# Seven-product output projection of a hybrid decoder layer: the order of the second round's products, of VectorE's steps at the change of rounds, and of the last two pairs

## The chip, the cores and the metric

One core of a Trainium2 chip runs one launch of the kernel. The metric is the device time in microseconds; three runs of the kernel before gave 846.16, 846.9 and 846.91, so its median is 846.9 us. A profiled execution is a run of its own, and its time is given beside these.

In the profile PE is TensorE's matrix multiplication, PEld its weight load, DVE is VectorE, ACT is ScalarE, POOL is GpSimd and SP is the engine that issues most loads.

## The reference, cut to what matters

A layer mixes tokens in three branches and then applies a SwiGLU feed-forward block. The change lies in the last line, for 512 tokens, 1024 channels and 2816 hidden units in float32:

```python
hf = rms_norm(x, ffn_norm_g[l]) @ w_ffn_in[l]
gt, up = jnp.split(hf, 2, axis=-1)
x = x + (jax.nn.silu(gt) * up) @ w_ffn_out[l]
```

## The kernel before, in words

A float32 operand is kept as two rounded parts, hi and lo, and a product of two operands as three matrix multiplications: hi by hi, hi by lo, lo by hi (`mm3`, L92). To split a weight block, ACT casts the hi part (L81) and then DVE subtracts it from the block for the lo part (L82). The hi parts lie in buffers `wh` and the lo parts in `wl`, three of each. `raw` (three buffers) holds a block as it was loaded, and `tt` (two buffers) holds sums of blocks.

The hidden units are done in two calls, of 12 and of 10 tiles of 128. In each, `ffn_in` makes the hidden activations and `ffn_out` (L806) multiplies them with the output weights. `ffn_out` takes the hidden tiles in pairs: six pairs in the first call, five in the second, which ends the kernel. A pair times its two rows of weights is a 2 by 2 block product, and it is done with seven products of half size in place of eight (Strassen and Winograd). The halves of the tokens and the halves of the output columns make four quarters of the output; `x(i, c)` is a 128-token tile `i` and a column half `c` of the running output. Each product writes two banks of PSUM with three matmuls each, so it takes six matmuls.

There are two rounds over all pairs of a call, since eight banks do not hold all sums:

- Round one (L827) makes products 1, 6 and 7 of each pair, into the banks p1, p6 and p7.
- Change of rounds (L845 to L856): ACT copies p1 out (L850), DVE adds p6 to it (L851) and gets s2; ACT writes s2 into the banks p5 (L852), as the start of product 5's sum. DVE adds p7 to the output (L854) and overwrites p7 with minus p7 minus s2 (L855), as the start of product 4's sum. The banks of p6 become p3, those of p7 become p4.
- Round two (L857) makes products 2, 3, 5 and 4 of each pair. Products 2 and 3 use the pair's raw second row of weights, split in one piece. I call that block R, with the pair's number behind it: R0, R1 and so on. Products 5 and 4 use sums that DVE forms (L865 to L867) and that are then split in one piece; I call that block S, likewise S0, S1. Of a pair's 24 matmuls twelve use R and twelve use S.
- After round two, `add` (L877) adds the banks to the output. In the last call the result goes into a new buffer `t` (six of them) and from there to memory by a DMA that ACT issues (L881). For two of the eight tiles ACT copies the bank out (L889) and POOL adds.

PE's instructions run in the order in which the program writes them. The others are put in order by a scheduler, engine by engine, by priorities: what stands in a `high_priority` block (the loads, splits and sums of weights) is put as early as the scheduler finds it ready; `issue_after` puts an instruction behind a named one of its engine. Each engine then works strictly through its row and waits at the first instruction that is not ready. A buffer is given out again once all that reads it is done.

## Time and profile before

| What | Value |
|---|---|
| median of 3 runs | 846.9 us (846.16 to 846.91) |
| the profiled execution, its own time | 846.77 us |
| its span, first to last instruction | 845.0 us |
| PE busy | 822.5 us, 97% of the span |
| DVE busy | 603.8 us, 71% |
| ACT busy | 396.3 us, 47% |
| POOL busy | 37.6 us, 4% |
| mean granted TensorE clock | 0.998 |

The profiled execution's own time is 1.77 us above its span, for what lies around the instructions. In a timeline each row gives the start and the duration in microseconds, then engine, line, operation and what it writes from what it reads; a bracket at its end names the idle time ahead of it on that engine and what ended it. A matmul row's duration is modelled and longer than the distance to the next one, since matmuls are pipelined. In a table by windows "x" is the number of instructions, and the DMA share is the mean busy share of the 16 DMA engines.

### The profile page before, as it was taken

The page shows a single profiled execution, that of the slowest core. Times are in us where ns is not written, and L with a number is a line of the kernel's source. Part 1 is how long each engine was busy: PE and PEld are TensorE (multiplying, and loading weights), DVE is VectorE, ACT ScalarE, POOL GpSimd, SP SyncE. Part 2 cuts the span into 40 slices and gives each one's busy share as a digit, 9 for nine tenths or more (in the row PEclk, how much of TensorE's full clock was granted, in tenths as well). Part 3 has the DMA queues.
Part 4 walks back from the last instruction along what each step waited for, and adds up shares of the span by engine and source line. Part 5 has one row for each costly group of instructions (what it writes and reads, how often), then busy time and mean ns, then how long its engine had stood idle before and what let it go on. Part 6 is the DMA issues. An engine that isn't in the chain of part 4 may idle for free. (4 is left out here: it accounts for less than half of the span.)

```text
span 845.0 us, 9697 instructions
## 1 busy us (share of the span) xinstructions
PE 822.5 (97%) x3727; PEld 682.4 (81%) x3727; DVE 603.8 (71%) x880; ACT 396.3 (47%) x583; POOL 37.6 (4%) x62
## 2 busy tenths in 40 slices
PE   6999999999999999999999999999998999999986
PEld 6888887888888888888888888888886888888864
DVE  5598799897899999774443456556698755566984
ACT  5336698886664222663342353333344323333441
POOL 3100010002100000000000120000000000000001
PEclk9999999999999999999999999999999999999999
DMA  7333114112113143142253133322355432323432
GB/s 250 103 100 96 55 50 150 50 56 95 50 50 100 55 145 100 53 148 99 100 184 115 50 100 100 100 100 88 112 173 185 164 99 100 101 88 112 162 125 100
DMA packets 71274, 90.11 MB, mean 107 GB/s; under 512 B 1920, under 2 KB 56380, under 8 KB 71228
## 3 DMA queue, kind: packets, MB, share of 16 engines
q1 hardware_dynamic: 70060, 87.39, 31.2%
q10 hardware_dynamic: 1168, 2.10, 0.6%
q8 instruction: 29, 0.48, 0.2%
q14 instruction: 17, 0.14, 0.1%
HBM read 87.39 MB, written 2.10 MB: 106 GB/s over the span
## 5 line engine op out<-in xcount | busy, mean ns | idle before, releaser
L90 PE MATMUL mm<-u,wh 128*128 128x512 f32 x1536 | 474.8, 390 | 0.0
L90 PEld LDWEIGHTS mm<-u,wh 128*128 128x128 f32 x1536 | 287.4, 188 | 59.4 <-DVE u L710 0.6
L90 PE MATMUL mm<-u,wl 128*128 128x512 f32 x768 | 299.2, 390 | 0.0
L81 ACT CAST wh<-raw 128x1024 fp32r<-128x1024 f32 (+1 forms) x154 | 146.9, 954 | 284.8 <-PE mm L90 219.2
L82 DVE TENSOR_TENSOR wl<-raw,wh 128x1024 fp32r<-128x1024 f32 (+1 forms) x152 | 168.4, 1109 | 61.9 <-ACT wh L81 61.5
L90 PEld LDWEIGHTS mm<-u,wl 128*128 128x128 f32 x768 | 144.2, 188 | 30.0
L502 DVE SCALAR_TENSOR_TENSOR cf<-cf,cols_w,cf 128x512 f32<-128x512 f32 x120 | 89.9, 749 | 3.7 <-ACT cf L500 1.2
L793 DVE TENSOR_TENSOR t<-mm,cf 128x512 f32<-128x512 f32 x22 | 15.2, 691 | 59.7 <-PE mm L90 59.7
L90 PE MATMUL mm<-m,wh 128*128 128x512 f32 x128 | 39.4, 389 | 0.0
L90 PE MATMUL mm<-wh,m 128*128 128x512 f32 x104 | 35.0, 392 | 4.1 <-DVE t L851 2.7
L81 ACT CAST wh<-tt 128x1024 fp32r<-128x1024 f32 x22 | 23.1, 1052 | 24.3 <-PE mm L90 24.3
L82 DVE TENSOR_TENSOR wl<-tt,wh 128x1024 fp32r<-128x1024 f32 x22 | 26.9, 1222 | 10.6 <-ACT wh L81 10.5
L791 DVE TENSOR_TENSOR t<-mm,cf 128x512 f32<-128x512 f32 x22 | 15.1, 688 | 24.8 <-PE mm L90 24.8
L90 PE MATMUL z<-wh,m 128*128 128x512 f32 x84 | 30.4, 396 | 2.0 <-DVE z L855 2.0
L90 PEld LDWEIGHTS mm<-m,wh 128*128 128x128 f32 x128 | 24.0, 188 | 4.9
L78 ACT ACTIVATE s<-s 128x384 f32<-128x384 f32 (+1 forms) x48 | 26.9, 561 | 1.2
L90 PEld LDWEIGHTS mm<-wh,m 128*128 128x128 f32 x104 | 19.5, 188 | 9.4 <-DVE t L851 3.5
L90 PE MATMUL mm<-m,wl 128*128 128x512 f32 x64 | 24.9, 389 | 0.0
L448 DVE SCALAR_TENSOR_TENSOR s<-z,s 128x384 f32<-128x384 f32 (+1 forms) x24 | 14.4, 598 | 11.6 <-ACT s L78 10.4
L78 ACT ACTIVATE t<-t 128x512 f32<-128x512 f32 x31 | 19.6, 631 | 3.7 <-DVE t L791 3.7
L717 POOL TENSOR_TENSOR cf<-cf,t 128x512 f32<-128x512 f32 x7 | 9.9, 1415 | 255.2 <-ACT t L715 255.0
L558 DVE TENSOR_TENSOR t<-mm,t 128x512 f32<-128x512 f32 x16 | 10.9, 689 | 14.0 <-PE mm L90 14.0
(257 smaller groups left out, 1070.3 us busy)
## 6 DMA issues: line engine op xcount, KB each, us to landing
raw<-in_w_in_dram SPq DMA_DIRECT2D x23, 1024.0 KB
raw<-in_w_ffn_in_dram SPq DMA_DIRECT2D x22, 1024.0 KB
raw<-in_w_ffn_out_dram SPq DMA_DIRECT2D x11, 1024.0 KB
raw<-in_w_ffn_out_dram SPq DMA_DIRECT2D x11, 512.0 KB
raw<-in_w_in_dram SPq DMA_DIRECT2D x10, 512.0 KB
raw<-in_w_o_dram SPq DMA_DIRECT2D x4, 1024.0 KB
raw<-in_w_ffn_out_dram SPq DMA_DIRECT2D x11, 256.0 KB
m<-in_x_dram SPq DMA_DIRECT2D x8, 256.0 KB
```

The source lines that it names most:

```text
L78: table(nc.scalar.activation(o, i, f, **kw))
L81: (copy or nc.scalar.copy)(hi, src)
L82: (sub or nc.vector.tensor_sub)(lo, src, hi.bitcast(F32))
L90: nc.tensor.matmul(o, lhsT, rhs, start=start, stop=stop, skip_group_check=True)
L448: marks.append(nc.vector.scalar_tensor_tensor(t, z, 0.0, t, ALU.max, ALU.add))
L502: nc.vector.scalar_tensor_tensor(y, pad[:, n:n + S], w(n), y, ALU.mult, ALU.add)
L558: nc.vector.tensor_mul(s[0], y, s[0])
L717: nc.gpsimd.tensor_add(sumsq, sumsq, s)
L791: nc.vector.tensor_mul(g, pg[0], rstd[0])
L793: nc.vector.tensor_mul(u, pu, rstd[0])
```

## The change

Round two's order on PE: products 2 and 3 of a pair are followed by products 5 and 4 of the pair before it, not of the same pair. In the last call, the last two pairs are done product by product: 5 of both, then 3, 4 and 2 of both. The last pair's R and S are split there into buffers `u`, which held the input of `ffn_in` and are free by then, and not into `wh` and `wl`.

At the change of rounds, ACT copies p7 out first (`s7`), DVE overwrites p7 at once and adds the copy to the output later; all of this but the last addition gets a high priority. From the second pair on, the sums of a pair are put behind a named instruction of DVE: behind the overwriting of the second bank of p7, and then behind the sums of the pair before it.

At the end, all additions are DVE's and stand in place: no buffer `t`, no copy by ACT, no addition by POOL, and the DMAs read the output's own tiles. The additions come in the order 5, 3, 4, 1 in the last call, and 1, 3, 5, 4 in the first.

```diff
--- before.py
+++ after.py
@@ -812,12 +812,17 @@
                 a = [t[:, i * P:(i + 1) * P] for t in h[j][p]]
                 mm3(banks[i], a, w, start and j == 0, stop and j == n - 1)
 
-        def parts(src):
+        def parts(src, tag=None):
+            if tag:
+                with tc.high_priority():
+                    return [split(src[:, i], tag) for i in range(src.shape[1])]
             hi, lo = wsplit(src)
             return [(hi[:, i], lo[:, i]) for i in range(src.shape[1])]
 
-        def sums(fn):
-            with tc.high_priority():
+        def sums(fn, *behind):
+            with tc.high_priority(), ExitStack() as stack:
+                for ins in behind:
+                    stack.enter_context(tc.issue_after(ins))
                 t = alloc("tt", (P, 2, S))
                 fn(t[:, 0], t[:, 1])
             return t
@@ -844,16 +849,22 @@
 
         x = lambda i, c: x1[c][:, i, :]
         p5 = [psum(tag) for tag in ("z", "o")]
-        s2 = [tmp(), tmp()]
+        s2, s7 = [tmp(), tmp()], []
+        with tc.high_priority(offset=PRIO):
+            for i in range(2):
+                s1 = tmp()
+                nc.scalar.copy(s1, p1[i])
+                nc.vector.tensor_add(s2[i], p6[i], s1)
+                nc.scalar.copy(p5[i], s2[i])
+            for i in range(2):
+                s7.append(tmp())
+                nc.scalar.copy(s7[i], p7[i])
+                change = nc.vector.scalar_tensor_tensor(p7[i], p7[i], -1.0, s2[i], ALU.mult,
+                                                        ALU.subtract)
         for i in range(2):
-            s1 = tmp()
-            nc.scalar.copy(s1, p1[i])
-            nc.vector.tensor_add(s2[i], p6[i], s1)
-            nc.scalar.copy(p5[i], s2[i])
-        for i in range(2):
-            nc.vector.tensor_add(x(i + 2, 1), p7[i], x(i + 2, 1))
-            nc.vector.scalar_tensor_tensor(p7[i], p7[i], -1.0, s2[i], ALU.mult, ALU.subtract)
+            nc.vector.tensor_add(x(i + 2, 1), s7[i], x(i + 2, 1))
         p3, p4 = [psum("mm") for _ in range(2)], p7
+        todo, behind, formed = [], [], []
         for j in range(n):
             with tc.high_priority():
                 w = alloc("raw", (P, 2, 2, S))
@@ -864,36 +875,52 @@
             def t14(t1, t4):
                 nc.vector.tensor_sub(t1, b12, b11)
                 nc.vector.tensor_sub(t4, b22, b21)
-                nc.vector.tensor_sub(t4, t4, t1)
-
-            two, three = parts(w[:, 1])
-            t1, t4 = parts(sums(t14))
-            order = [(2, two, p1, False), (3, three, p3, True), (5, t1, p5, False),
-                     (4, t4, p4, False)]
-            for k in range(4) if j < n - 1 else (1, 2, 3, 0):
-                p, part, banks, start = order[k]
-                products(j, p, part, banks, start, True)
+                formed[:] = [nc.vector.tensor_sub(t4, t4, t1)]
+
+
+
+            tag = "u" if last and j == n - 1 else None
+            two, three = parts(w[:, 1], tag)
+            t1, t4 = parts(sums(t14, *behind), tag)
+            behind = [formed.pop().ins if j else change.ins]
+            todo.append([(j, 2, two, p1, False, True), (j, 3, three, p3, True, True),
+                         (j, 5, t1, p5, False, True), (j, 4, t4, p4, False, True)])
+            if last and j >= n - 2:
+                now = [at[2:] for at in todo[:-1]] if j == n - 2 else [
+                    [at[k] for at in todo[-2:]] for k in (2, 1, 3, 0)]
+            else:
+                now = [todo[-1][:2]] + [at[2:] for at in todo[:-1]]
+                if j == n - 1:
+                    now.append(todo[-1][2:])
+            for group in now:
+                for args in group:
+                    products(*args)
+            todo = todo[-1:] if not last or j < n - 2 else todo[-2:]
 
         def add(i, c, p, final, op=nc.vector.tensor_add):
-            y = tmp() if last and final else x(i, c)
-            op(y, x(i, c), p)
+            op(x(i, c), x(i, c), p)
             if last and final:
-                nc.scalar.dma_start(out[i * P:(i + 1) * P, c * S:(c + 1) * S], y)
-
-        for i in range(2):
-            add(i, 1, p3[i], False)
-        for i in range(2):
-            add(i, 1, p5[i], True)
-            if last:
-                s1 = tmp()
-                nc.scalar.copy(s1, p5[i])
-                add(i + 2, 1, s1, True, nc.gpsimd.tensor_add)
-            else:
+                nc.scalar.dma_start(out[i * P:(i + 1) * P, c * S:(c + 1) * S], x(i, c))
+
+        def add1():
+            for i in range(2):
+                add(i, 0, p1[i], True)
+
+        def add3():
+            for i in range(2):
+                add(i, 1, p3[i], last)
+
+        def add4():
+            for i in range(2):
+                add(i + 2, 0, p4[i], True, nc.vector.tensor_sub)
+
+        def add5():
+            for i in range(2):
                 add(i + 2, 1, p5[i], True)
-        for i in range(2):
-            add(i + 2, 0, p4[i], True, nc.vector.tensor_sub)
-        for i in range(2):
-            add(i, 0, p1[i], True)
+                add(i, 1, p5[i], False)
+
+        for fn in (add5, add3, add4, add1) if last else (add1, add3, add5, add4):
+            fn()
 
     j0 = 0
     for c, n in enumerate((12, 10)):
```

Below are three places of the built programs, in the last call of `ffn_out`. The first is DVE's row at the change of rounds. `z` with the lower number is the first bank of p7, `mm` are banks of p6, `wl` from a `raw` is the lo part of an R and `wl` from a `tt` that of an S. Before, from R0's lo part on:

```order
L82 TENSOR_TENSOR wl_1156_6396<-raw_1154_6393,wh_1155_6395 128x1024
L867 TENSOR_TENSOR tt_1163_6437<-tt_1163_6437 128x512
L82 TENSOR_TENSOR wl_1159_6404<-tt_1157_6399,wh_1158_6403 128x1024
L851 TENSOR_TENSOR t_1148_6377<-mm_1112_6211,t_1150_6379 128x512
L865 TENSOR_TENSOR tt_1169_6475<-raw_1166_6469 128x512
L866 TENSOR_TENSOR tt_1169_6475<-raw_1166_6469 128x512
L82 TENSOR_TENSOR wl_1162_6434<-raw_1160_6431,wh_1161_6433 128x1024
L867 TENSOR_TENSOR tt_1169_6475<-tt_1169_6475 128x512
L851 TENSOR_TENSOR t_1149_6378<-mm_1113_6212,t_1151_6383 128x512
L854 TENSOR_TENSOR v_663_3713<-z_1114_6213,v_663_3713 128x512
L855 SCALAR_TENSOR_TENSOR z_1114_6213<-z_1114_6213,t_1148_6377 128x512
L854 TENSOR_TENSOR v_663_3713<-z_1115_6214,v_663_3713 128x512
```

And now, from R0's lo part on:

```order
L82 TENSOR_TENSOR wl_1160_6404<-raw_1158_6401,wh_1159_6403 128x1024
L857 TENSOR_TENSOR t_1150_6381<-mm_1114_6215,t_1152_6383 128x512
L82 TENSOR_TENSOR wl_1163_6412<-tt_1161_6407,wh_1162_6411 128x1024
L857 TENSOR_TENSOR t_1151_6382<-mm_1115_6216,t_1153_6387 128x512
L862 SCALAR_TENSOR_TENSOR z_1116_6217<-z_1116_6217,t_1150_6381 128x512
L865 TENSOR_TENSOR v_663_3713<-t_1154_6391,v_663_3713 128x512
L82 TENSOR_TENSOR wl_1166_6430<-raw_1164_6427,wh_1165_6429 128x1024
L862 SCALAR_TENSOR_TENSOR z_1117_6218<-z_1117_6218,t_1151_6382 128x512
L876 TENSOR_TENSOR tt_1167_6433<-raw_1164_6427 128x512
L877 TENSOR_TENSOR tt_1167_6433<-raw_1164_6427 128x512
L865 TENSOR_TENSOR v_663_3713<-t_1155_6394,v_663_3713 128x512
L878 TENSOR_TENSOR tt_1167_6433<-tt_1167_6433 128x512
```

Before, the sums of pairs 1 and 2 and R1's lo part stand between the two additions of p6 and ahead of all that frees p7. Now both additions and the first bank of p7 come ahead of R1's lo part, and the sums of pair 1 behind the second bank of p7.

The second place is ACT's row at the same change. Before, from R0's cast to S1's:

```order
L81 CAST wh_1155_6395<-raw_1154_6393 128x1024
L850 COPY t_1150_6379<-mm_1110_6209 128x512
L81 CAST wh_1158_6403<-tt_1157_6399 128x1024
L81 CAST wh_1161_6433<-raw_1160_6431 128x1024
L852 COPY z_1146_6375<-t_1148_6377 128x512
L850 COPY t_1151_6383<-mm_1111_6210 128x512
L852 COPY o_1147_6376<-t_1149_6378 128x512
L81 CAST wh_1164_6441<-tt_1163_6437 128x1024
```

And now, from R0's cast to S1's:

```order
L81 CAST wh_1159_6403<-raw_1158_6401 128x1024
L856 COPY t_1152_6383<-mm_1112_6213 128x512
L81 CAST wh_1162_6411<-tt_1161_6407 128x1024
L856 COPY t_1153_6387<-mm_1113_6214 128x512
L858 COPY z_1148_6379<-t_1150_6381 128x512
L861 COPY t_1154_6391<-z_1116_6217 128x512
L81 CAST wh_1165_6429<-raw_1164_6427 128x1024
L858 COPY o_1149_6380<-t_1151_6382 128x512
L861 COPY t_1155_6394<-z_1117_6218 128x512
L81 CAST wh_1168_6437<-tt_1167_6433 128x1024
```

The copy of p1's second bank moved from behind R1's cast to ahead of it, and the two copies of p7 stand on either side of that cast.

The third place is DVE's row a little later, around the lo parts of pairs 1 and 2. Before, from S1's lo part on:

```order
L82 TENSOR_TENSOR wl_1165_6442<-tt_1163_6437,wh_1164_6441 128x1024
L855 SCALAR_TENSOR_TENSOR z_1115_6214<-z_1115_6214,t_1149_6378 128x512
L865 TENSOR_TENSOR tt_1175_6513<-raw_1172_6507 128x512
L866 TENSOR_TENSOR tt_1175_6513<-raw_1172_6507 128x512
L867 TENSOR_TENSOR tt_1175_6513<-tt_1175_6513 128x512
L82 TENSOR_TENSOR wl_1168_6472<-raw_1166_6469,wh_1167_6471 128x1024
L82 TENSOR_TENSOR wl_1171_6480<-tt_1169_6475,wh_1170_6479 128x1024
L865 TENSOR_TENSOR tt_1181_6551<-raw_1178_6545 128x512
```

And now, from the sums of pair 1 on:

```order
L876 TENSOR_TENSOR tt_1167_6433<-raw_1164_6427 128x512
L877 TENSOR_TENSOR tt_1167_6433<-raw_1164_6427 128x512
L865 TENSOR_TENSOR v_663_3713<-t_1155_6394,v_663_3713 128x512
L878 TENSOR_TENSOR tt_1167_6433<-tt_1167_6433 128x512
L876 TENSOR_TENSOR tt_1173_6471<-raw_1170_6465 128x512
L877 TENSOR_TENSOR tt_1173_6471<-raw_1170_6465 128x512
L82 TENSOR_TENSOR wl_1169_6438<-tt_1167_6433,wh_1168_6437 128x1024
L82 TENSOR_TENSOR wl_1172_6468<-raw_1170_6465,wh_1171_6467 128x1024
L878 TENSOR_TENSOR tt_1173_6471<-tt_1173_6471 128x512
```

R2's lo part moved from a place five rows behind S1's to the row right behind it, and two of the three sums of pair 2 stand ahead of both. In the program as built, R2 is split into the buffer that R1 had, and likewise every later R that is split into `wh` and `wl`; S1 goes into the buffer of R0, and a later S into that of the S two pairs earlier. Before, the three buffers went round, so that an R took the buffer of the S two pairs earlier.

## The prediction

> **What bounds the kernel now.** I read the page first, then the list of what PE waited for, and then the timeline of each engine at the places that this list names. The page's first lines:
>
> ```profile
> span 845.0 us, 9697 instructions
> PE 822.5 (97%) x3727; PEld 682.4 (81%) x3727; DVE 603.8 (71%) x880; ACT 396.3 (47%) x583; POOL 37.6 (4%) x62
> ```
>
> PE is busy for 97% of the span, and the change takes no matmul away. It can gain only where PE stands still, and behind PE's last matmul. The list of PE's waits (total, times, longest, in us) names these places:
>
> ```profile
> PE mm L296 <- DVE a L294: 4.3, 2, 4.1
> PE mm L90 <- DVE t L851: 2.7, 2, 2.0
> PE o L229 <- DMA rows_g<-in_mix_norm_g_dram: 2.3, 1, 2.3
> PE z L90 <- DVE z L855: 2.0, 2, 1.0
> PE mm L90 <- ACT t L850: 1.5, 1, 1.5
> ```
>
> Two of them (L296, L229) lie at the kernel's start. The other three, 6.2 us, all come from the change of rounds. PE's timeline there, first call and then second:
>
> ```profile
> 639.85 0.39 PE L90 MATMUL mm<-wh,m 128*128 128x512 f32 x1
> ...
> 648.92 0.40 PE L90 MATMUL mm<-wh,m 128*128 128x512 f32 x1
> ...
> 654.37 0.39 PE L90 MATMUL mm<-wh,m 128*128 128x512 f32 x1
> ```
> ```profile
> 805.33 0.39 PE L90 MATMUL mm<-wh,m 128*128 128x512 f32 x1
> ...
> 807.63 0.50 PE L90 MATMUL mm<-wh,m 128*128 128x512 f32 x1 [1.46 <-ACT t L850]
> 807.97 0.40 PE L90 MATMUL mm<-wl,m 128*128 128x512 f32 x1
> ...
> 809.93 0.50 PE L90 MATMUL mm<-wh,m 128*128 128x512 f32 x1 [0.64 <-DVE t L851]
> ...
> 814.76 0.39 PE L90 MATMUL mm<-wh,m 128*128 128x512 f32 x1
> ...
> 836.31 0.39 PE L90 MATMUL mm<-wh,b 128*128 128x512 f32 x1
> ```
>
> The rows at 639.85, 648.92 and 654.37 are the first matmuls of pairs 0, 1 and 2. An undisturbed pair takes 654.37 - 648.92 = 5.45 us for 24 matmuls, 0.227 each. Pair 0 takes 9.07 in the first call and 814.76 - 805.33 = 9.43 in the second. So the changes of rounds cost 3.62 and 3.98, 7.60 together, which is more than the idle time: behind an idle stretch the second matmul comes 0.34 after the first (807.63 to 807.97), 0.11 more than the pitch. From 814.76 to the last matmul at 836.31 there are 95 steps of 0.227: nothing is lost there.
>
> What is left is the end, 845.0 - 836.31 = 8.69 us behind the last matmul's start:
>
> ```profile
> 834.05 0.38 ACTq L881 DMA_DIRECT2D out_dram<-t  x1
> ...
> 838.04 1.26 POOL L879 TENSOR_TENSOR t<-v,t 128x512 f32<-128x512 f32 x1 [1.61 <-issue]
> 838.56 1.47 DVE L879 TENSOR_TENSOR t<-v,mm 128x512 f32<-128x512 f32 x2 [0.81 <-DMA out_dram<-t]
> 839.34 2.35 ACTq L881 DMA_DIRECT2D out_dram<-t  x5
> ```
> ```profile
> 834.00:835.00 1.00, 1.00 (x6) 0.80 (x6) 0.70 (x2) 0.52 (x1) 0.00 (x0) 1.00 0.05 18
> 835.00:836.00 1.00, 1.00 (x6) 0.84 (x5) 0.00 (x0) 0.06 (x1) 0.86 (x1) 1.00 0.63 244
> ...
> 843.00:844.00 1.00, 0.00 (x0) 0.00 (x0) 0.00 (x0) 0.00 (x0) 0.00 (x0) 0.50 0.50 184
> 844.00:845.00 1.00, 0.00 (x0) 0.00 (x0) 0.00 (x0) 0.00 (x0) 0.00 (x0) 0.50 0.00 0
> ```
>
> POOL's second addition ends at 839.30, and ACT's row of DMAs, five of eight, starts at 839.34 behind it. DVE's last two additions, ready when product 2 ended, wait for a buffer `t` that a DMA still reads. In the windows the last two columns are the DMA share and the rate: the first tile, issued at 834.05, moves from about 834.95 on, 0.9 later, and takes 0.05 + 0.63 = 0.68. The last tile's transfer ends in the middle of 843 to 844, about 1.5 ahead of the span's end.
>
> **The changes of rounds, step by step.** ACT and DVE there, second call:
>
> ```profile
> 801.45 1.05 ACT L81 CAST wh<-raw 128x1024 fp32r<-128x1024 f32 x1 [1.62 <-PE z L90]
> 802.41 0.57 ACT L850 COPY t<-mm 128x512 f32<-128x512 f32 x1
> 802.88 1.05 ACT L81 CAST wh<-tt 128x1024 fp32r<-128x1024 f32 x1
> 805.53 1.05 ACT L81 CAST wh<-raw 128x1024 fp32r<-128x1024 f32 x1 [1.60 <-PE z L90]
> ...
> 807.00 0.58 ACT L850 COPY t<-mm 128x512 f32<-128x512 f32 x1
> ```
> ```profile
> 804.51 1.22 DVE L82 TENSOR_TENSOR wl<-tt,wh 128x1024 fp32r<-128x1024 f32 x1
> 805.64 0.69 DVE L851 TENSOR_TENSOR t<-mm,t 128x512 f32<-128x512 f32 x1
> 806.24 0.69 DVE L865 TENSOR_TENSOR tt<-raw 128x512 f32<-128x512 f32 x1
> ...
> 809.18 0.69 DVE L851 TENSOR_TENSOR t<-mm,t 128x512 f32<-128x512 f32 x1
> ```
>
> These rows give the prices. A cast takes 1.05 and frees ACT for the next after 0.96, a copy 0.57 and 0.47. A lo part takes 1.22 and the next starts after 1.13, any other step of DVE 0.69 and 0.60. From one engine to the next I take 0.05. A matmul's result is there 0.39 behind its start. They also name the fault: the copy of p1's second bank (807.00) stood behind R1's cast, which waits for round one's last matmul, and the second L851 (809.18) behind three sums and a lo part.
>
> Now the new order, in the second call's clock. R0's cast ends at 802.50, and DVE goes: R0's lo 802.54, first addition 803.68, S0's lo 804.28, second addition 805.42, first bank of p7 806.02, the late addition 806.62, R1's lo 807.22 to 808.44, second bank of p7 808.36 to 809.05. ACT has copied p1's second bank by 804.41 and p7's first by 805.48 (its last matmul starts four steps ahead of 805.33), and casts R1 from 805.53 as before. So pair 0's products 2 and 3 run from 805.33 to 808.05 without a wait: every bank that they need is free at the latest at 806.11, for a matmul due at 807.37. R1's twelve follow at 808.05; the second of them, due at 808.28, needs R1's lo at 808.49: 0.21, and 0.11 for the restart. S0's twelve start at 811.09; p7's second bank, due two microseconds later, was free at 809.05.
>
> Then the sums. DVE takes pair 1's from 808.96 with the other late addition among them, to 811.45, and two of pair 2's to 812.65. S1's cast waits for the sums: 811.50 to 812.55. R2's cast stands behind it on ACT, 812.46 to 813.51, and R2's lo behind S1's lo on DVE: 812.60, 813.73, done at 814.95. PE is ready for R2 at 811.09 + 2.72 = 813.81 and its second matmul at 814.04, but gets the lo part at 815.00: 0.96, and 0.11. This wait is new. It costs 0.32 + 1.07 = 1.39 of the 3.98, so the second call's change gains 2.59.
>
> In the first call R0's cast stood at 635.93, as far ahead of 639.85 as here (3.92 against 3.88), so the same steps give the same 1.39. There R3 follows after S1. DVE reaches R3's lo only behind S2's lo and three sums, 14.30 behind R0's first matmul, and ends it at 15.52; PE wants it at 15.22: 0.35 and 0.11. R4 and R5 find DVE idle, each with 0.37 to spare: from the end of the R before it, 0.05 + 1.05 + 0.05 + 1.22 + 0.05 = 2.42, against 2.72 - 0.16 + 0.23 = 2.79 until PE needs it. Loss 1.85 of 3.62, gain 1.77. In the second call R3 and S3 have S2's products in between, S3's lo ends some 0.1 ahead of its matmul, and the last pair's split has buffers of its own: nothing.
>
> The loads move with the sums, since they wait for a buffer `raw`. The last one was issued here, and its data had come by the end of the second row:
>
> ```profile
> 808.70 0.37 SPq L860 DMA_DIRECT2D raw<-in_w_ffn_out_dram  x1
> ```
> ```profile
> 812.00:813.00 1.00, 0.96 (x5) 0.45 (x3) 0.93 (x1) 0.04 (x1) 0.00 (x0) 1.00 0.89 365
> ```
>
> That is 4.2 us. Now it waits for pair 1's second sum, about 810.3, and lands about 814.5. Its cast to `u` stands ahead of S2's on ACT; S2's lo is needed at 820.5 and takes 2.8 from there, so 3 us are to spare. The two more copies on ACT and the reads of p7 by ACT lie beside PE's work and cost nothing; without that cover each would be 0.57.
>
> **The end.** PE's row ends 2.59 earlier by the second call alone. From the last matmul's start: result 0.39, to DVE 0.05, addition 0.69, to ACT 0.05, 0.9 to the first byte, 0.68, and 1.5 to the span's end, 4.26 in all. The first bank of product 2 is ready 0.68 earlier, so its transfer is just out of the way. The six other tiles are done by then: products 5, 3 and 4 of both pairs end 8.2, 5.4 and 2.7 ahead, and DVE needs 2.4, 1.2 and 1.2 for them, with nothing else in its row. Gain 8.69 - 4.26 = 4.43. The nearest rows bound it: with the DMA issued later by one other transfer, 0.68 less; with the 1.5 at the end cut to half, 0.7 more. The Trainium skill, "DMA: Bandwidth & Descriptors", section "Anatomy of one DMA", gives a fixed part of about 2.0 us and 436 GB/s beside it: an estimate by that page is 2.6 for a tile of 256 KB where my rows give 0.9 + 0.68 + 1.5 = 3.1, and the time would be 0.5 lower; the section fits another issuing path, and I keep the rows.
>
> **Sum.** 2.59 + 1.77 + 4.43 = 8.79, so the span goes from 845.0 to 836.2. The profiled execution took 846.77, 1.77 above its span and 0.13 below the median of 846.9. On the median the forecast is 838.1, and I say 838.0. A change of 0.2% either way, 1.7 us, is about what a measurement of this kernel can tell from none.
>
> **Rivals.** *R's buffer bites on every block.* Each later R goes into the buffer of the R before it, so it has 2.79 us where 2.42 are needed; before, it had a product group more. For it: a single DVE step (0.60 to 1.13) in the way is more than the 0.37 left. Against it: DVE's row is short from the middle of the round on. R3, R4 and R5 of the first call and S3 of the second at up to 0.9 each give 3 more, 841. The Trainium skill, "Perfetto Trace Analysis", section "Optimization Strategy", holds that the same gap coming back on the engine that should be full can mean too few buffers; no gap comes back in before's rounds.
>
> *No wait inside round two.* If the scheduler's row lets DVE and ACT run a little ahead of my sum, 1.39 and 1.85 fall away: 834.8. Against it: the order of S1's and R2's lo parts is fixed.
>
> *One half gives nothing.* If other steps take the place of the waits at both changes, or if the last DMAs are held up as before, the other half is left: 846.9 - 4.4 = 842.5. For it: the copies of p7 are new links in the chain. Against it: all of them have over a microsecond to spare.
>
> *Slower.* Serial splits at every R: sums (3 x 0.60), S's cast and lo, then R's lo, all behind the release of R's buffer, are 1.8 + 1.05 + 1.13 + 1.22 + 0.15 = 5.35 from the end of an R to the next. Less 2.79 that is a wait of 2.56 and 0.11, 2.7 on five R's (R2 to R5 and R2): 13.4 where I count 2.6 for them, so 838.0 + 10.8 = 848.8. It decides for slower from a mean wait of 2.4 per R on. Against it: the sums and S's cast wait for no release of R.
>
> **Chances.** Forecast 0.67, with 835.5 to 840.5 as its own range; R's buffer 0.12; no wait 0.07; one half 0.10; slower 0.04. The range 835.0 to 841.2 takes in the first and nearly all of the second. All but the last are faster by over 0.2%: 0.95; within 0.2% 0.01, a weak form of the last; slower 0.04.
>
> **What would show it.** In the new profile: no wait of PE for the copies of p1 or the additions of p6; a wait of about 1 us of PE for a lo part at R2 in both calls, and a small one at R1 and at the first call's R3; the last DMA issued about 1.2 us behind the last matmul's start and the span's end 4.3 behind it. The prediction is wrong if PE waits at every R, if a wait for p7's banks or a load appears, or if the last matmul isn't about 4.4 earlier.

## The result and the profile after

The changed kernel takes 837.88 us (median of 4 runs, 837.32 to 838.15) where the kernel before takes 846.66 (4 runs). The ratio is 0.9896, with a 95% interval of 0.9879 to 0.9913: faster by 8.8 us. The forecast was 838.0, with a range of 835.0 to 841.2. The profiled execution took 837.62.

The page of the changed kernel begins:

```profile
span 835.9 us, 9695 instructions
PE 821.9 (98%) x3727; PEld 681.7 (82%) x3727; DVE 604.1 (72%) x884; ACT 397.0 (47%) x587; POOL 35.1 (4%) x60
```

The list of what PE waited for (total, times, longest, in us):

```profile
PE mm L296 <- DVE a L294: 4.5, 2, 4.3
PE o L229 <- DMA rows_g<-in_mix_norm_g_dram: 2.4, 1, 2.4
PE mm L90 <- DVE wl L82: 1.9, 3, 0.8
PE mm L90 <- DVE t L82: 1.4, 2, 1.2
```

The three entries of before at the change of rounds (DVE `t`, ACT `t`, DVE `z`, 6.2 us) are gone. In their place stands one new entry, three waits for a lo part `wl`, 1.9 us. PE's timeline shows where they are:

```profile
639.61 0.39 PE L90 MATMUL mm<-wh,m 128*128 128x512 f32 x1
...
642.71 0.50 PE L90 MATMUL mm<-wl,m 128*128 128x512 f32 x1
643.04 0.63 PE L90 MATMUL mm<-wh,m 128*128 128x512 f32 x2
...
648.05 0.39 PE L90 MATMUL mm<-wh,m 128*128 128x512 f32 x1
649.27 0.50 PE L90 MATMUL mm<-wl,m 128*128 128x512 f32 x1 [0.83 <-DVE wl L82]
...
655.22 0.50 PE L90 MATMUL mm<-wl,b 128*128 128x512 f32 x1 [0.21 <-DVE wl L82]
```
```profile
803.38 0.39 PE L90 MATMUL mm<-wh,m 128*128 128x512 f32 x1
...
805.87 0.61 PE L90 MATMUL mm<-wh,m 128*128 128x512 f32 x2
806.53 0.50 PE L90 MATMUL mm<-wl,m 128*128 128x512 f32 x1
...
811.89 0.39 PE L90 MATMUL mm<-wh,m 128*128 128x512 f32 x1
813.10 0.50 PE L90 MATMUL mm<-wl,m 128*128 128x512 f32 x1 [0.82 <-DVE wl L82]
...
830.77 1.52 PE L90 MATMUL mm<-u,b 128*128 128x512 f32 x6
```

639.61 and 803.38 are R0's first matmuls in the two calls. The second matmul of an R is the first that reads its lo part. At R2 it comes 813.10 - 811.89 = 1.21 after the first one, where the pitch is 0.227. The bracket says 0.82 and not 0.98, because it counts from the modelled end of the matmul ahead; distances between starts are the safer measure, and I use them from here on. The short waits at R1 (805.87 plus one pitch to 806.53, so 0.43) get no bracket at all for the same reason.

The last of the six matmuls of the row at 830.77 starts five pitches later, at 831.90. The end behind it, on DVE, on ACT, and in the windows (last two columns: DMA share and rate):

```profile
831.64 1.37 DVE L901 TENSOR_TENSOR v<-v,mm 128x512 f32<-128x512 f32 x2 [1.35 <-PE mm L90]
```
```profile
824.20 9.19 ACTq L903 DMA_DIRECT2D out_dram<-v  x8
```
```profile
833.00:834.00 1.00, 0.00 (x0) 0.00 (x0) 0.01 (x1) 0.00 (x0) 0.00 (x0) 1.00 0.75 291
834.00:835.00 1.00, 0.00 (x0) 0.00 (x0) 0.00 (x0) 0.00 (x0) 0.00 (x0) 1.00 0.61 234
835.00:835.90 0.90, 0.00 (x0) 0.00 (x0) 0.00 (x0) 0.00 (x0) 0.00 (x0) 1.00 0.00 0
```

The eight DMAs are spread over 9.19 us (before, five of eight went out together at the very end). Only the two tiles of product 2 are left behind the last matmul; their transfers run one behind the other and fill 0.75 + 0.61 = 1.36 us of the DMA engines' time, twice the 0.68 of before's first tile.

Where the 9.1 us between the spans (845.0 and 835.9) come from, cut at R0's two first matmuls and at the last matmul:

| Stretch | before | after | gain | forecast |
|---|---|---|---|---|
| to R0, first call | 639.85 | 639.61 | 0.24 | 0 |
| R0, first call, to R0, second call | 165.48 | 163.77 | 1.71 | 1.77 |
| R0, second call, to the last matmul's start | 30.98 | 28.52 | 2.46 | 2.59 |
| behind the last matmul's start | 8.69 | 4.00 | 4.69 | 4.43 |

The 0.24 in the first row isn't the change's. Over the profiled executions in the table of the next section R0's first matmul stands between 639.46 and 640.55. The scatter is there by PE's 60th matmul, some 16 us into the span, and hardly grows behind it; the long wait at L296, which lies ahead of that point, took between 3.4 and 4.8 us. So profiled executions are compared below by the span from R0 on: 845.0 - 639.85 = 205.15 for before, 835.9 - 639.61 = 196.29 for after, a gain of 8.86 where the sum said 8.79.

Two single runs further below, one of end_only (2145.68 us) and one of best_fixed (1181.86 us), lie far above all others of their kernels and are left out of the medians.

### The profile page after: what moved, and what is told of

Its sections match the earlier page's. It is cut to its first block, busy times and chain, and to the rows that moved or that the text cites. A ratio compares the mean times of both kernels' runs of the same rounds, so it can differ in the third digit from the quotient of the medians.

```text
span 835.9 us, 9695 instructions
## 1 busy us (share of the span) xinstructions
PE 821.9 (98%) x3727; PEld 681.7 (82%) x3727; DVE 604.1 (72%) x884; ACT 397.0 (47%) x587; POOL 35.1 (4%) x60
## 4 chain that ended last, share of the span: by engine, by line
PE 91%; DVE 6%; issue 1%; ACT 1%; DMA 1%; SPq 0%; DVEq 0%
PE mm L90 77%; PE z L90 11%; PE o L90 3%; DVE wl L82 2%; DMA m<-in_x_dram 1%; DVE cf L502 0%; DVE tt L877 0%; DVE tt L876 0%; ACT wh L81 0%; PE mm L705 0%; DVE tt L878 0%; DVE t L283 0%; DVE t L82 0%; DVE z L862 0%; DVE m L375 0%
## 5 line engine op out<-in xcount | busy, mean ns | idle before, releaser
L90 PE MATMUL mm<-wl,m 128*128 128x512 f32 x52 | 20.7, 398 | 1.7 <-DVE wl L82 1.6
```

Of the source, the lines that this page charges most:

```text
L90: nc.tensor.matmul(o, lhsT, rhs, start=start, stop=stop, skip_group_check=True)
```

## The experiments

Two questions were open. Which of the parts bring the gain: the new order at the change of rounds, the lag of products 5 and 4 by a pair, or the end? And are the new waits the price of the lag, of the late additions in DVE's row, or of the single buffer of the R's? All twelve runs:

| Kernel | median us | ratio to before, 95% interval | span from R0 on | gain in it |
|---|---|---|---|---|
| before | 846.5 to 846.9 in the calls | | 205.15 | |
| changed kernel | 837.88 | 0.9896 [0.9879, 0.9913] | 196.29 | 8.86 |
| lag_only | 846.18 | 0.9997 [0.9988, 1.0007] | 204.84 | 0.31 |
| end_only | 843.96 | 0.997 [0.9959, 0.9982] | | |
| end_only_look | 844.07, one run | | 202.07 | 3.08 |
| change_only | 839.14 | 0.9912 [0.9897, 0.9927] | 197.89 | 7.26 |
| change_inplace | 836.46 | 0.9873 [0.9857, 0.989] | 195.61 | 9.54 |
| old_end | 838.22 | 0.99 [0.9884, 0.9917] | 196.25 | 8.90 |
| r2_own | 837.98 | 0.9897 [0.9882, 0.9912] | 196.34 | 8.81 |
| late_add | 836.55 | 0.988 [0.9866, 0.9895] | 195.12 | 10.03 |
| no_lag | 835.89 | 0.9871 [0.9855, 0.9888] | 194.61 | 10.54 |
| no_lag_late | 835.74 | 0.9866 [0.9851, 0.9881] | 193.98 | 11.17 |
| no_lag_late_3first | 834.23 | 0.9855 [0.984, 0.987] | 192.83 | 12.32 |
| best_fixed | 834.26 | 0.985 [0.9834, 0.9867] | 192.79 | 12.36 |

The intervals are some 0.3% wide, about 2.7 us, and only those of no_lag_late_3first and best_fixed lie wholly below the changed kernel's. The smaller steps therefore rest on the waits and spans in the traces.

### One part at a time

**change_only**: before with the new change of rounds and the sums behind named instructions. Order on PE and end are before's.

```diff
-        for i in range(2):
-            nc.vector.tensor_add(x(i + 2, 1), p7[i], x(i + 2, 1))
-            nc.vector.scalar_tensor_tensor(p7[i], p7[i], -1.0, s2[i], ALU.mult, ALU.subtract)
+        with tc.high_priority(offset=PRIO):
...
+                nc.scalar.copy(s7[i], p7[i])
+                change = nc.vector.scalar_tensor_tensor(p7[i], p7[i], -1.0, s2[i], ALU.mult,
+                                                        ALU.subtract)
...
-            t1, t4 = parts(sums(t14))
+            t1, t4 = parts(sums(t14, *behind))
+            behind = [formed.pop().ins if j else change.ins]
```

> The kernel before with only the change of rounds done anew: ACT copies p7 out, DVE overwrites it at once and adds the copy later, all but that addition at high priority, and the sums of pair 1 and on stand behind it. Products 5 and 4 follow 2 and 3 of the same pair as before, and the end is as before. Theory (DVE's and ACT's order is the whole gain at the changes, and the order of products on PE adds nothing to it): p7's second bank is free about 1 us ahead of product 4's second bank, S1's lo part comes 0.2 to 0.3 late, R2 has a product group more time; PE loses about 0.3 in each call where before loses 3.6 and 4.0, so 7.0 less: 839.8. Rival (products 5 and 4 one pair behind is what covers the freeing of p7): PE still waits about 1 to 1.5 in each call for p7 or S0, and the gain is 4 to 5: 842 to 843.

It took 839.14: 7.6 us of the 8.8 by itself. Its loss against the pitch is only 0.26 in the first call and 0.30 in the second, one short wait at S1 in each; R2 doesn't wait.

**lag_only**: before with the lag, and nothing else.

```diff
-            order = [(2, two, p1, False), (3, three, p3, True), (5, t1, p5, False),
-                     (4, t4, p4, False)]
...
+            now = [todo[-1][:2]] + [at[2:] for at in todo[:-1]]
+            if j == n - 1:
+                now.append(todo[-1][2:])
...
+            todo = todo[-1:]
```

> The kernel before with only the order of products on PE changed: 5 and 4 of a pair behind 2 and 3 of the next pair, in both calls up to the last pair; change of rounds, sums and end as before. Theory (the order of DVE and ACT is what counts): the waits for the copy of p1's second bank (1.5) and for the second addition of p6 (0.6 to 2) stay, the wait for p7 (1.0) goes, and waits for the lo parts of R1, R2 and R3 of about 1 each come: between 1 us less and 3 us more than before, 845.7 to 850. Rival (the order of products is what gains): 2 to 4 less than before at the changes, 843 to 845.

It took 846.18, within 0.2% of before. In its list of PE's waits, before's `z` from L855 is gone, and the other two stand as they were. The waits of about 1 us that were expected for the lo parts of R1, R2 and R3 did not come:

```profile
PE mm L90 <- DVE t L851: 2.7, 2, 2.0
...
PE mm L90 <- ACT t L850: 1.5, 1, 1.5
```

So the lag does hide the wait for p7: from R0 on, its last matmul (833.80) stands 194.34 behind R0's first (639.46), before's 836.31 - 639.85 = 196.46, a gain of 2.12. But its end is 844.3 - 833.80 = 10.50 long, 1.81 more than before's. Product 5 is now six matmuls nearer to the last one, and the chain of DVE, ACT and POOL that starts from it begins later. Its first output DMA goes out 0.89 ahead of the last matmul's start (832.91) and not 2.26 ahead (834.05 before), which is 1.37 of it. The rest is not explained. What is left is 0.31.

**end_only**: before with the additions in place, all on DVE, in the old order.

```diff
-            y = tmp() if last and final else x(i, c)
-            op(y, x(i, c), p)
+            op(x(i, c), x(i, c), p)
...
-            if last:
-                s1 = tmp()
-                nc.scalar.copy(s1, p5[i])
-                add(i + 2, 1, s1, True, nc.gpsimd.tensor_add)
-            else:
-                add(i + 2, 1, p5[i], True)
+            add(i + 2, 1, p5[i], True)
```

> The kernel before with only the end changed: the final additions are all DVE's and in place, no buffer t, no copy by ACT, no addition by POOL; products keep their old order. Theory (the end is worth its own term, whatever the rounds do): PE's row ends as before, 836.3 in the span. The old order leaves products 3, 5, 4 and 2 of the last pair only 1.36 us apart, so ten additions follow each other at 0.60 from about 832.0 to 837.7, and eight transfers of 0.68 from about 834.0 on end near 840; with 1.5 behind them the span is 841 to 842, the time 842.5 to 843.8, a gain of 3 to 4. Rival (the end's gain needs the last two pairs product by product): the additions pile up and the gain is under 1.5, 845.5 or more. Second rival (the end is bound by the DMA queue itself, not by t and POOL): no gain, 846.7.

It took 843.96, a gain of 2.8, a little less than expected. Its trace is that of one more execution:

> One more profiled execution of before with in-place additions by DVE at the end, to see where its 2.8 us come from: the last DMA issued 1 to 1.5 us behind the last matmul's start and the span's end 5 to 6 us behind it, where before has 8.69. Rival: the end is as long as before, and the 2.8 us come from elsewhere (for example the POOL additions that no longer run beside DVE's).

DVE's row at its end (each row's second addition included):

```profile
832.26 1.36 DVE L878 TENSOR_TENSOR v<-v,mm 128x512 f32<-128x512 f32 x2 [1.09 <-PE mm L90]
833.62 1.28 DVE L878 TENSOR_TENSOR v<-v,z 128x512 f32<-128x512 f32 x2
834.82 1.28 DVE L878 TENSOR_TENSOR v<-v,o 128x512 f32<-128x512 f32 x2
836.02 1.27 DVE L878 TENSOR_TENSOR v<-v,z 128x512 f32<-128x512 f32 x2
837.21 1.27 DVE L878 TENSOR_TENSOR v<-v,mm 128x512 f32<-128x512 f32 x2
```

Ten additions run without a hole for 6.2 us and end at 838.48, 1.89 behind the last matmul's start (836.59); the span ends at 842.2, 5.6 behind it, as the theory said, though the last DMA goes out somewhat later than the 1 to 1.5 it named. The waits for buffers and for POOL are gone. What ends last is now the row of transfers. Its first windows and its last, with the DMA share and the rate at the end:

```profile
835.00:836.00 1.00, 1.00 (x6) 0.83 (x5) 1.00 (x2) 0.00 (x0) 0.00 (x0) 1.00 0.79 307
836.00:837.00 1.00, 0.98 (x5) 0.48 (x3) 1.00 (x3) 0.00 (x0) 0.00 (x0) 1.00 1.05 408
...
840.00:841.00 1.00, 0.00 (x0) 0.00 (x0) 0.00 (x0) 0.00 (x0) 0.00 (x0) 1.00 0.45 170
```

DVE sends a tile every 0.60 us, and a transfer takes 0.68, so the eight run without a hole from about 835.2 to the second half of 840 to 841. The last tile, issued at about 838.5, would by itself be through at 838.5 + 0.9 + 0.68 = 840.1. In the old order the first of the ten additions can begin only 4.3 us ahead of the last matmul, and DVE's row and the transfers' row both start from there.

### What the end's gain is made of

**change_inplace**: change_only and end_only together, still in the old order.

> Before with the new change of rounds, the sums behind, and in-place additions by DVE at the end, in the old order of products and additions. If the end's gain comes from the in-place additions as well as from the order (alone on the kernel before they brought 2.8 us), it takes 839.1 - 2.7 = 836.4 us, and the order of the last two pairs is worth only some 0.5 more. Rival: on top of the new change of rounds the in-place additions bring nothing: 839.1 us, and the order alone brings the 3.2 us down to the kernel without the lag.

It took 836.46, as the theory said: in the medians the two gains add (from R0 on 0.8 is missing, 9.54 against 7.26 + 3.08). This kernel has neither the lag nor the new order of the last two pairs, and is 1.4 us faster than the changed kernel in median, 0.7 from R0 on; the two intervals overlap.

**old_end**: the changed kernel with before's `t` buffers, ACT's copies and POOL's additions, in the new order of products and additions.

```diff
-            op(x(i, c), x(i, c), p)
+            y = tmp() if last and final else x(i, c)
+            op(y, x(i, c), p)
...
-                add(i + 2, 1, p5[i], True)
+                if last:
+                    s1 = tmp()
+                    nc.scalar.copy(s1, p5[i])
+                    add(i + 2, 1, s1, True, nc.gpsimd.tensor_add)
+                else:
+                    add(i + 2, 1, p5[i], True)
```

> The changed kernel with the old additions at the end: new buffers t, product 5's lower tiles copied out by ACT and added by POOL; the last two pairs stay product by product, product 5 first. Theory of the prediction (the buffers t and POOL's additions held the last DMAs): with product 5 done 8 us ahead of the last matmul POOL's additions and the first DMAs are long over when product 2 ends, so the old additions cost nothing here: 837.9 to 838.3; then the order of the products alone brings the end's 4.7. Rival (in-place additions are the gain, the order only spreads the transfers): DVE's last additions still wait for buffers or POOL, and the end is 1.5 to 3 longer, 839.4 to 841.

It took 838.22, and from R0 on 196.25 against 196.29: no difference. With the products in groups, POOL's additions are over more than five microseconds ahead of the last matmul. So the order of the last two pairs brings the end's 4.7 us alone; additions in place bring 2.8 where the old order stands, and nothing beside the new one. Two remedies for the same hold-up are not two gains.

### What the new waits are made of

**no_lag**: the changed kernel without the lag; the last two pairs stay product by product.

```diff
-                now = [at[2:] for at in todo[:-1]] if j == n - 2 else [
+                now = [] if j == n - 2 else [
...
-                now = [todo[-1][:2]] + [at[2:] for at in todo[:-1]]
-                if j == n - 1:
-                    now.append(todo[-1][2:])
+                now = [todo[-1]]
```

> The changed kernel with products 5 and 4 directly behind 2 and 3 of the same pair; the last two pairs of the last call stay product by product; all else as changed. Theory (with DVE's order fixed the lag only costs, since it leaves R2 and R3 too little time): PE waits for no R, and about 0.3 in each call for S1's lo part; against the changed kernel 1.5 less in the first call and 1.1 in the second, span 833.2, time 835.2. Rival (the lag covers the freeing of p7 and S0): PE waits 1 to 1.5 more in each call at product 4 of pair 0, and the time is 838 to 840, not faster than the changed kernel.

It took 835.89, 2.0 us less than the changed kernel (1.68 from R0 on). The waits at R1, R2 and R3 are gone. S1 waits briefly in each call, and in the last two pairs of the second call S3's lo part comes late (0.55, and 0.11 for the restart) and so does S4's (0.32 and 0.11):

```profile
818.66 0.39 PE L90 MATMUL z<-wh,b 128*128 128x512 f32 x1
819.44 0.50 PE L90 MATMUL z<-wl,b 128*128 128x512 f32 x1 [0.39 <-DVE wl L82]
```

So nearly all of the gain lies in the first call: from R0 to R0 it takes 162.13 where the changed kernel takes 163.77, and from the second R0 to the last matmul 28.43 against 28.52. The 1.1 us expected from the second call did not come. S3 has six groups of twelve matmuls ahead of it with the lag and without, and its lo part ends 17.37 behind R0's first matmul here (819.39 - 802.02), 17.88 in the changed kernel (821.26 - 803.38). There PE had already lost 1.41 at R1 and R2 and so came late enough; here it comes in time and has to wait.

Why the lag costs at R2 is seen in DVE's row, which is the same with and without it up to R2's lo part. The second call of the changed kernel, R1's lo part, S1's and R2's:

```profile
805.26 1.22 DVE L82 TENSOR_TENSOR wl<-raw,wh 128x1024 fp32r<-128x1024 f32 x1
...
808.20 0.69 DVE L865 TENSOR_TENSOR v<-t,v 128x512 f32<-128x512 f32 x1
...
810.00 0.69 DVE L877 TENSOR_TENSOR tt<-raw 128x512 f32<-128x512 f32 x1
810.68 1.23 DVE L82 TENSOR_TENSOR wl<-tt,wh 128x1024 fp32r<-128x1024 f32 x1
811.82 1.22 DVE L82 TENSOR_TENSOR wl<-raw,wh 128x1024 fp32r<-128x1024 f32 x1
```

and of change_only, which has no lag, PE's R0 first and then the same three rows of DVE:

```profile
801.77 0.39 PE L90 MATMUL mm<-wh,m 128*128 128x512 f32 x1
```
```profile
803.65 1.22 DVE L82 TENSOR_TENSOR wl<-raw,wh 128x1024 fp32r<-128x1024 f32 x1
...
809.07 1.22 DVE L82 TENSOR_TENSOR wl<-tt,wh 128x1024 fp32r<-128x1024 f32 x1
810.21 1.22 DVE L82 TENSOR_TENSOR wl<-raw,wh 128x1024 fp32r<-128x1024 f32 x1
```

Counted from R0's first matmul, R2's lo part is done at 811.82 + 1.22 - 803.38 = 9.66 with the lag and at 810.21 + 1.22 - 801.77 = 9.66 without (in no_lag itself it is 9.66 too). PE's wish differs: with the lag the order is R0, R1, S0, R2, and R2's second matmul is due 3 x 2.72 + 0.23 = 8.39 behind R0's first, 8.72 with R1's wait of 0.33 in it: 0.05 from engine to engine added, it is 0.99 late, as measured. Without the lag the order is R0, S0, R1, S1, R2, and it is due 2.72 later. S0's split is ready long before, and the lag puts it behind R1, which isn't.

**late_add**: the changed kernel with the two late additions behind the last pair's sums.

```diff
-        for i in range(2):
-            nc.vector.tensor_add(x(i + 2, 1), s7[i], x(i + 2, 1))
...
+        with tc.issue_after(behind[0]):
+            for i in range(2):
+                nc.vector.tensor_add(x(i + 2, 1), s7[i], x(i + 2, 1))
```

> The changed kernel with one thing moved: the two late additions of p7's copies to the output stand behind the last pair's sums instead of in DVE's row between p7 and R1's lo part and among pair 1's sums. The lag and the buffers stay. Theory (the new waits at R1, R2 and R3 come from the length of DVE's row behind the change of rounds): R1's lo part comes 0.6 earlier, pair 1's sums and with them the casts and lo parts of S1 and R2 1.0 to 1.2 earlier; PE's wait at R1 goes, that at R2 falls from 0.8 to 0.1 or 0.2, that at R3 in the first call goes; against the changed kernel 1.5 and 1.1 less in the two calls, 835.2 to 835.6. Rival (R's single buffer sets these waits): R2's cast can't start before R1's matmuls end, the waits at R2 and R3 stay, and only R1's 0.3 in each call goes: 837.2.

It took 836.55, between the two. DVE's row is 1.2 shorter there, R1 no longer waits, and at R2 the second matmul comes 0.53 behind the first, not 1.21:

```profile
810.98 0.39 PE L90 MATMUL mm<-wh,m 128*128 128x512 f32 x1
811.51 0.50 PE L90 MATMUL mm<-wl,m 128*128 128x512 f32 x1
```

What was gained there, about 1.0 in each call, is partly given back: R4 of the first call now waits 0.15 and 0.11, with a late addition right ahead of its lo part (658.20 and 658.80), and in the second call S3 and S4 lose 0.51 together, with the late additions between the last pair's lo parts. R3 of the first call, whose wait was expected to go, still waits 0.38: R2 still waits for its lo part, and from there to R3's lo part DVE's row has the same steps as in the changed kernel, 5.95 us. From R0 on 1.17 is left.

**r2_own**: the changed kernel, in which R2 of the last call has buffers `u` of its own.

```diff
-            two, three = parts(w[:, 1], tag)
+            two, three = parts(w[:, 1], "u" if last and j in (2, n - 1) else None)
```

> The changed kernel, but in the last call R2 is also split into two free buffers u of its own, in two halves, instead of into the one buffer of R1. Theory (the wait at R2 is the order on ACT and DVE, which the scheduler set by R2's buffer coming free late): with a buffer at hand R2's cast and lo parts stand ahead of pair 1's sums, R2's wait of 0.8 goes, R1's lo part stays where it was or comes up to 0.6 later; 0.5 to 1.2 less than the changed kernel, 836.7 to 837.4. Rival (the buffer itself is not what counts, the sums are late anyway): the wait moves on to S1's or S2's lo part, and the time is the changed kernel's, 837.9.

It took 837.98, no gain, and 196.34 from R0 on. R2's wait is gone in the second call, and a wait of the same size stands at S4:

```profile
823.39 0.73 PE L90 MATMUL z<-u,a 128*128 128x512 f32 x2 [0.75 <-DVE u L82]
```
```profile
822.05 0.68 DVE L865 TENSOR_TENSOR v<-t,v 128x512 f32<-128x512 f32 x1
822.65 1.29 DVE L82 TENSOR_TENSOR u<-tt,u 128x512 fp32r<-128x512 f32 x2
```

The scheduler made another row of it and put a late addition right ahead of S4's lo parts. So this run doesn't cleanly separate the buffer from the row: it shows that the wait isn't a gain to be had from a buffer alone. That the buffer isn't what R2 waits for is seen in the changed kernel's own ACT rows: R2's cast follows S1's, which waits for DVE's sums, while R1's last matmul, which frees the buffer, had started at 808.94.

```profile
809.60 1.05 ACT L81 CAST wh<-tt 128x1024 fp32r<-128x1024 f32 x1 [3.92 <-DVE tt L878]
810.55 1.05 ACT L81 CAST wh<-raw 128x1024 fp32r<-128x1024 f32 x1
```

R3 of the first call is another case. Its cast does start only when R2's last matmul (651.67) is done:

```profile
652.14 1.06 ACT L81 CAST wh<-raw 128x1024 fp32r<-128x1024 f32 x1 [1.18 <-PE mm L90]
```
```profile
653.95 1.22 DVE L82 TENSOR_TENSOR wl<-raw,wh 128x1024 fp32r<-128x1024 f32 x1
```

DVE begins the lo part 0.75 behind the cast's end, since three sums stand ahead of it, so DVE's row sets PE's wait of 0.37. Whether the scheduler would have put the lo part ahead of these sums if the buffer had come free sooner is not shown.

### A version that beats both

**no_lag_late** is no_lag with late_add's edit. **no_lag_late_3first** has product 3's groups ahead of product 5's in the last two pairs, and product 3's additions first; it sends two of the eight tiles before product 5 is added to them, so its output leaves out that part. **best_fixed** adds product 5 to them and then sends them, and computes all of the output. The diff shows best_fixed against no_lag_late.

```diff
-                    [at[k] for at in todo[-2:]] for k in (2, 1, 3, 0)]
+                    [at[k] for at in todo[-2:]] for k in (1, 2, 3, 0)]
...
-                add(i, 1, p3[i], last)
+                add(i, 1, p3[i], False)
...
-                add(i, 1, p5[i], False)
+                add(i, 1, p5[i], True)
...
-        for fn in (add5, add3, add4, add1) if last else (add1, add3, add5, add4):
+        for fn in (add3, add5, add4, add1) if last else (add1, add3, add5, add4):
```

> The same without the change of group order at the end (product 5's group first, as in the changed kernel). If the waits for the last pair's lo parts in the end phase (0.39 + 0.11 us at S3, 0.2 + 0.2 at S4 in the kernel without the lag) are set by the order of the groups, they stay: 834.9 to 835.4 us, 0.6 to 1.1 above the kernel with product 3's group first. Rival: the late additions caused them too; then 834.0 to 834.5, and the group order is worth nothing.

> Three things on the changed kernel: no lag of products 5 and 4, the late additions behind the last pair's sums, and in the last two pairs product 3 of both ahead of product 5 of both (so R3 and R4 are used first, and S3 has a product group more time). Theory: S1's wait of 0.15 to 0.2 in each call and the waits of 0.4 to 0.6 at S3 and S4 that the kernel without the lag has all go; PE stands still nowhere in round two, its last matmul starts near 829.0 in the span, 4.0 to 4.3 before its end: span 833.0 to 833.3, time 834.4 to 834.9. Rival (additions of product 5 now pile up behind those of product 3, and the late additions hold S4's lo part): the end grows or PE waits by 1 or more, and the time is that of the kernel without the lag, 835.9, or more.

> The changed kernel without the one-pair lag of products 5 and 4, with the two late additions behind the last pair's sums, and at the end of the last call product 3's group before product 5's, its additions too; the output tiles that both add to are sent behind product 5's additions, so that the whole output is computed. If the lag, the late additions and the group order are what is left of avoidable waiting in round two (2.0 us from the kernel without the lag, 1.3 from the late additions, less what the two share), it takes 833.9 to 834.8 us, about 3.3 less than the changed kernel. Rival: the 834.2 us of the kernel that left product 5 out of two tiles came from that omission; then 835.2 or more.

no_lag_late took 835.74, more than expected: the late additions moved out of the change of rounds into the last pair, and S1's two waits (0.55 in all) went while one at S4 of 0.92 took the place of those at S3 and S4. no_lag_late_3first took 834.23 and best_fixed 834.26, so the omission had no part in the time. From R0 on they agree within 0.04, and product 3's group first is worth 193.98 - 192.79 = 1.19: product 3 needs only R3 and R4, and S3 and S4 get 2.7 us more. In best_fixed's list nothing of round two is left:

```profile
PE mm L296 <- DVE a L294: 3.4, 1, 3.4
PE o L229 <- DMA rows_g<-in_mix_norm_g_dram: 3.2, 1, 3.2
PE mm L90 <- DVE t L82: 1.4, 2, 1.2
```

Its interval, 0.9834 to 0.9867, lies below the changed kernel's (0.9879 to 0.9913): 3.6 us less in median, 3.5 in the span from R0 on.

## Why the prediction was right, step by step

**The changes of rounds** went as worked out. None of the waits for p1's copy, p6's additions or p7's banks came back. The three new waits stand where they were put, and with the sizes given. In distances between starts less the pitch: R1 0.15 and 0.21 (forecast 0.21), R2 0.99 and 0.98 (0.96), the first call's R3 0.37 (0.35), each with 0.11 for the restart. That follows from DVE's row: with R0's first matmul as zero, R1's lo part was to end at 808.44 - 805.33 = 3.11 and ended at 805.26 + 1.22 - 803.38 = 3.10; R2's at 9.62, and it was 9.66. Adding up the row that the engine will work through, step by step, with start-to-start prices, held to a few hundredths of a microsecond over nine microseconds.

**The second call's term** was 0.13 too large, 2.59 against 2.46: the named waits make 1.41 of the loss and not 1.39, and some 0.1 is spread over steps too small to list.

**The load** of the last pair's weights was to land some 4.2 us behind its issue and keep nobody waiting on PE. It came 0.6 later than said: its cast could start 813.15 - 803.38 = 9.77 behind R0's first matmul, where 814.5 - 805.33 = 9.2 was the forecast. It held up ACT, and PE not:

```profile
813.15 0.62 ACT L81 CAST u<-raw 128x512 fp32r<-128x512 f32 x1 [1.55 <-DMA raw<-in_w_ffn_out_dram]
```

S2's cast, behind it on ACT, started at 813.73, when its sums were just formed (DVE ends them at 813.65).

**The end** was 4.00 where 4.26 was said. The last addition ends 833.01 - 831.90 = 1.11 behind the last matmul's start, as in the sum (0.39 + 0.05 + 0.69). The transfers follow each other without a hole, and the second ends at about 834.7, 1.2 ahead of the span's end; that step was taken as 1.5. From the last DMA's issue, about 833.05, to the span's end it is 2.85. The Trainium skill, "DMA: Bandwidth & Descriptors", section "Anatomy of one DMA", gave an estimate of 2.6 for this stretch and the rows of before 3.1: the measurement lies midway. The cause given for the gain, though, is only half the story: the prediction credited the order and the additions in place together, and old_end shows that beside the new order the second does nothing.

**The sum** came closer than its terms. The two changes together gained 0.19 less than forecast and the end 0.26 more, so they nearly cancel; that the median lies only 0.1 from the forecast is partly luck, and less than the runs differ among themselves (837.32 to 838.15).

**The rivals.** R's single buffer was no bound on every block. Casts of the changed kernel do wait for it (R3's above), but PE's waits at R1 and R2 are for DVE's row, the one at R3 too with what was said above, and at R4 and R5 PE doesn't wait. The rule quoted there (the Trainium skill, "Perfetto Trace Analysis", section "Optimization Strategy": the same gap coming back can mean too few buffers) could have pointed to the buffers now, since waits at R1 and R2 come back in both calls; the runs say otherwise, as late_add takes away R1's wait and 0.68 of R2's without touching the buffers, and r2_own, with a buffer more, gains nothing. no_lag alone would not settle it: without the lag a later R takes the buffer of an S (R4's cast of the first call, at 656.75, waits for `PE z`), so there the buffers go round as they did before the change. *No wait inside round two* didn't happen here, but it is what best_fixed has; its price of 3.2 us was nearly what the three edits behind it brought (3.5). *One half gives nothing* fails for the whole. Of the parts, the lag alone gives nothing. In *Slower* the mean wait per R that decides should read 2.3, (846.9 - 838.0 + 2.6) / 5, and not 2.4; nothing hangs on it.

**What the prediction didn't ask** is what each part is for. It counted the new waits as the price of the change as a whole. The runs show that they are the price of the lag, and that the lag has no gain left to set against it: it hides the wait for p7 (2.1 us in lag_only), and the new order on DVE and ACT removes that same wait at its source. In the second call no_lag gives that price back at S3 and S4 (1.09 us), until product 3's group goes first (1.19 in best_fixed). The changed kernel is faster in spite of its first part.

## What to carry to other kernels

When two parts of a change cure the same wait, time each alone and leave one out: the second may bring no more gain and keep its cost (here 1.7 to 2 us for the lag). Where an engine's row at a change of phase is full, order the consumer's work so that what is ready early is used first, and push whatever nobody waits for (here two additions) to where the row has room; then look at what stands next behind its new place. In the last stretch, order the products so that their results leave one group at a time.

## What the runs showed of the hardware

- Behind an idle stretch of PE the second matmul came 0.33 to 0.34 us behind the first, not 0.227, whether PE had waited 0.15 us (S1 in change_only) or 2.2 us (before, 644.09): 0.11 for each wait, short or long.
- The same code ahead of the edits scattered by 1.1 us between profiled executions (R0's first matmul at 639.46 to 640.55), and 1.0 of it was there 16 us into the span. Differences under a microsecond between two spans mean little until that is taken off.
- Two 256 KB tiles one behind the other filled 1.36 us of the DMA engines' time, twice one alone (0.68); the 0.9 us from issue to the first byte of the second were hidden behind the first.
